# Token-number scatters moved into the loop over further blocks, and the last norm ahead of that loop, in a decoder layer with a mixture of experts

## The chip, the cores and the metric

The kernel runs on one core of a Trainium2 chip. The metric is device microseconds of one execution; the time of a kernel is the median of its runs. The engines are named as in the profile: PE (TensorE, matrix products), PEld (its weight loads), DVE (VectorE), ACT (ScalarE), POOL (GpSimd) and SP (SyncE, which issues most DMAs). L268 is the line of a recording helper through which most instructions go, so instructions are told apart by the names of their tiles.

## The reference

One layer of a decoder over 1024 tokens of width 1024 (and 16 learned ones ahead of them): a normalisation, four token mixers, an output projection, a normalisation, a mixture of experts, and a last normalisation. The change lies in the mixture of experts and behind it:

```
def _hier_moe(x, w_grp, b_grp, w_rt, b_rt, w_gate, w_up, w_down):
    ...
    g_sel = jnp.argmax(g_logit, -1)
    ...
    top_val, top_idx = lax.top_k(e_logit, TOP_K_INNER)
    w = jax.nn.softmax(top_val, -1) * p_grp
    e_idx = g_sel[:, None] * EXPERTS_PER_GROUP + top_idx
    ...
    for e in range(N_EXPERTS):
        hid = jax.nn.silu(xf @ w_gate[e]) * (xf @ w_up[e])
        y = y + gate[:, e:e + 1] * (hid @ w_down[e])
...
    h = _layer_norm(DN_ALPHA * h + moe_out, ln2_g[l], ln2_b[l])
return h[:, N_META:]
```

Each token takes two of 16 experts. All tensors are float32; the last normalisation scales by `ln2_g` and adds `ln2_b`.

## The kernel before

**The experts.** After the routing each expert has a first block of up to 192 tokens (`CAP`). `Experts` goes through the 16 experts one after the other. POOL gathers the expert's token rows from DRAM (`xg<-h1d,ix`, two gathers of 96 rows by an indirect DMA, four buffers). PE transposes them (`py<-ident,xg`), ACT and DVE split them into a high and a low part (`xT`), PE multiplies by the gate and up weights (`pg`), ACT and DVE form the hidden layer (`sg`, `th`, `su`) and split it into `hdh` (ACT) and `hdl` (DVE), and PE multiplies by the down weights (`py`). ACT copies the product to `ey`, and SP stores it in the result table `ys` in DRAM (`ys<-ey`, one store for each expert, two for the last two). The weights come in pieces of 512 KB (`raw`), issued by SP as buffers come free; ACT rounds each piece to its high part (`s4h`, `mT0h` and so on), and DVE or POOL subtracts for the low part (`s4l`, `mT0l`).

**Further blocks.** Where an expert has more than 192 tokens, the rest is done by `expert` in a device loop behind the 16 experts (L3016), once for each further block. The number of blocks, `nov`, is worked out on the device. With the inputs of this case it is 0, and no pass of the loop appears in the trace. A pass reads token numbers from the table `ids` in DRAM. `Routing.rest` fills that table with 16 indirect scatters on POOL (`ids<-tki,si`, 128 numbers each); each of them waits until the one before has landed, since all write one table. Behind them it writes a row of 16 numbers by an IOTA on POOL (`oj`), and DVE works out from it which blocks follow (`sl<-inc,oj` and eleven small instructions to `nov`).

**The end.** `ahead` gathers, for five of the eight groups of 128 tokens, the result of each token's first expert (`y<-ys,slot`, all from experts 0 to 14, so that it can run while expert 15 is computed) and adds it to the residual, times its weight. After the loop `finish` gathers the eight second results (`z`) and the three first ones that are left (`x`). DVE adds (L2880, with the sums of the rows; L2849 for the three), ACT squares with sums, takes the root and normalises, POOL multiplies by `ln2_g`, DVE adds `ln2_b`, SP stores. The eighth group is done in two halves.

**What sets the order.** The recording layer `Order` fixes the order of instructions on PE, DVE, ACT and POOL from the order in which generators yield; each engine runs its row in order, so what waits holds up all that stands behind it. `rest` runs beside the experts from the third on, `ahead` when 15 experts are stored. `finish` has an order of its own behind the loop. A program orders SP. The loop is a point at which all engines meet.

## Time and profile before

| | us |
|---|---|
| runs (three) | 1714.13, 1709.41, 1715.12 |
| median | 1714.13 |
| profiled execution | 1709.09 |
| its span | 1707.4 |
| PE busy | 1558.3 (91%) |
| PEld busy | 1320.4 (77%) |
| DVE busy | 1130.8 (66%) |
| ACT busy | 753.0 (44%) |
| POOL busy | 463.0 (27%) |

The span runs from the first to the last instruction; the profiled execution took 1.7 us more than its span. The experts fill about 1365 to 1640 us of it, `ahead`, the loop's empty start and `finish` the rest. Busy shares are means over the whole program, so the stretch in question has to be read by itself.

### The profile page before, as it was taken

What the parts mean: (1) busy time and instruction counts of PE and PEld (TensorE: products, weight loads), DVE (VectorE), ACT (ScalarE), POOL (GpSimd) and SP (SyncE); (2) the same over time, 40 slices, a digit from 0 to 9 for tenths busy, and PEclk for the clock granted to TensorE, in tenths of its full rate; (3) what the DMA queues carried; (4) which work ended last, traced back from release to release, by engine and by line L of the source; (5) the groups of instructions that cost most, each with busy time, mean ns of one, the idle gap of its engine ahead of it and who ended that gap; (6) DMA issues with size and microseconds to landing.
All of it is one profiled execution on the core that took longest, in us unless ns stands there. A gap on an engine that the chain in (4) does not pass through costs nothing. (4 is left out here: it accounts for less than half of the span.)

```text
span 1707.4 us, 27539 instructions
## 1 busy us (share of the span) xinstructions
PE 1558.3 (91%) x9899; PEld 1320.4 (77%) x9899; DVE 1130.8 (66%) x2545; ACT 753.0 (44%) x1519; POOL 463.0 (27%) x578
## 2 busy tenths in 40 slices
PE   4999998999999999999999999988999899699950
PEld 3999898888887777778787777766888778689840
DVE  8345765744589888865565588477576586477558
ACT  4344444445544454425444334331211367467634
POOL 5222227821111111232221221157200223301026
PEclk9999999999999999999999999999999899899985
DMA  7875444342322233262210541377223688699764
GB/s 242 250 215 153 144 141 115 98 121 72 102 69 75 68 96 102 90 191 75 59 35 17 142 120 49 105 242 244 71 87 112 185 237 269 174 283 291 222 195 179
DMA packets 224555, 244.84 MB, mean 143 GB/s; under 512 B 39531, under 2 KB 172557, under 8 KB 224417
## 3 DMA queue, kind: packets, MB, share of 16 engines
q1 hardware_dynamic: 218016, 222.08, 42.9%
q0 software_dynamic: 6400, 20.98, 4.4%
q8 instruction: 79, 1.29, 0.3%
q14 instruction: 60, 0.48, 0.1%
HBM read 168.98 MB, written 74.03 MB: 142 GB/s over the span
## 5 line engine op out<-in xcount | busy, mean ns | idle before, releaser
L268 PE MATMUL pj<-hTl,wh 128*128 128x512 f32 (+3 forms) x1184 | 432.6, 365 | 1.0 <-DVE hTl L268 1.0
L268 PE MATMUL pj<-hTh,wh 128*128 128x512 f32 (+3 forms) x1184 | 432.2, 365 | 0.0
L268 PE MATMUL pj<-hTh,wl 128*128 128x512 f32 (+3 forms) x1184 | 428.5, 362 | 0.0
L268 POOL TENSOR_TENSOR wl<-wr,wh 128x256 fp32r<-128x256 f32 (+1 forms) x177 | 138.0, 796 | 420.3 <-ACT wh L268 415.6
L268 PEld LDWEIGHTS pj<-hTh,wh 128*128 128x128 f32 (+1 forms) x1184 | 223.7, 189 | 26.4 <-issue 2.0
L268 PEld LDWEIGHTS pj<-hTl,wh 128*128 128x128 f32 (+1 forms) x1184 | 223.6, 189 | 26.4 <-issue 1.6
L268 PEld LDWEIGHTS pj<-hTh,wl 128*128 128x128 f32 (+1 forms) x1184 | 223.9, 189 | 23.5 <-issue 1.4
L268 ACT COPY pe<-pj 128x384 f32<-128x384 f32 (+3 forms) x84 | 37.3, 444 | 119.6 <-PE pj L268 81.5
L268 DVE SCALAR_TENSOR_TENSOR sc<-rl,wi,sc 128x512 f32<-128x512 f32 (+3 forms) x77 | 59.8, 776 | 39.8 <-ACT rl L268 36.4
L268 ACT CAST wh<-wr 128x256 fp32r<-128x256 f32 (+1 forms) x240 | 85.1, 402 | 0.1
L268 ACT ACTIVATE pe<-pj 128x512 f32<-128x512 f32 x64 | 38.1, 595 | 100.7 <-PE pj L268 75.0
L268 POOL TENSOR_TENSOR h<-h,g 128x512 f32<-128x512 f32 x46 | 63.7, 1399 | 51.6 <-issue 32.2
L268 PE MATMUL pg<-xT,mT0h 128*128 128x384 f32 x208 | 64.0, 369 | 0.0
L268 POOL DMA_INDIRECT xg<-h1d,ix x32 | 34.3, 1071 | 109.0 <-PE py L268 100.8
L268 ACT ACT_TABLE_LOAD x46 | 59.0, 1283 | 5.8 <-DVE qk L268 2.6
L268 POOL TENSOR_TENSOR sc<-sc,band 128x256 f32<-128x256 f32 (+1 forms) x32 | 24.4, 764 | 121.2 <-DVE sc L268 82.8
L268 PE MATMUL pg<-xT,mT0l 128*128 128x192 f32 x208 | 54.5, 262 | 0.0
L268 DVE TENSOR_TENSOR mT0l<-raw,mT0h 128x1024 fp32r<-128x1024 f32 x36 | 43.4, 1222 | 15.6 <-ACT mT0h L268 15.5
L268 ACT COPY PT<-xb 128x512 f32<-128x512 f32 (+3 forms) x56 | 27.4, 489 | 55.0 <-PE xb L268 52.8
L268 DVE TENSOR_TENSOR xT<-py,xT 128x384 fp32r<-128x384 f32 x64 | 35.2, 553 | 23.3 <-ACT xT L268 23.2
L268 PEld LDWEIGHTS po<-v,PT 128*128 128x128 f32 x352 | 45.8, 191 | 5.7 <-ACT PT L268 2.5
L268 PE MATMUL po<-v,PT 128*128 128x64 f32 x352 | 47.2, 271 | 0.7 <-ACT PT L268 0.7
(638 smaller groups left out, 3779.8 us busy)
## 6 DMA issues: line engine op xcount, KB each, us to landing
wr<-in_w_in_dram SPq DMA_DIRECT2D x59, 512.0 KB
raw<-in_moe_w_gate_dram SPq DMA_DIRECT2D x32, 512.0 KB
raw<-in_moe_w_up_dram SPq DMA_DIRECT2D x32, 512.0 KB
raw<-in_moe_w_down_dram SPq DMA_DIRECT2D x32, 512.0 KB
gtd<-pe SPq DMA_DIRECT2D x52, 256.0 KB
g<-gtd SPq DMA_DIRECT2D x52, 256.0 KB
ys<-ey SPq DMA_DIRECT2D x14, 768.0 KB
ys<-zero SPq DMA_DIRECT2D x8, 960.0 KB
```

What stands on the lines that cost most here:

```text
L268: r = f(*args, **kw)
```

## The change

The scatters go from `Routing.rest` to the body of the loop, and with that are issued only if a pass runs; their numbers (`si`, `tki`) are kept in a pool that lives to the end. The IOTA stays in `rest`. The results of first blocks are now taken for all tokens without regard to the loop: a slot of a further block is replaced by slot 0 with weight 0 (`slot`, `wt`), and a second pair (`slox`, `wx`) holds it for the loop. `ahead` gathers and adds all eight groups of first results, in six buffers, into the residual's own tiles. `finish` runs ahead of the loop: the eight second gathers, adds, norms and stores. In it DVE does both the multiplication and the addition, ACT takes the mean, and POOL only gathers. A pass of the loop ends with `again`, which adds what the further block gave, norms and stores once more.

```diff
-AHEAD = 5
-LAG = 2
+AHEAD = 6
+FAR = 16384
...
+        a, b, so, fs = t("oa"), t("ob8"), t("so", 2), t("fs", 2)
+        nc.vector.tensor_scalar(fs, sf, float(NE * CAP), -float(FAR), op0=OP.is_ge, op1=OP.mult)
+        nc.vector.tensor_add(sf, sf, fs)
+        yield
...
+        nc.vector.tensor_copy(self.slot, fs)
+        nc.vector.tensor_scalar(fs, so, float(FAR), float(NSLOT - 1), op0=OP.add, op1=OP.min)
+        nc.vector.tensor_copy(self.slox, fs)
+        nc.vector.tensor_scalar(fs, so, 0.0, None, op0=OP.is_ge)
...
-        for j in range(8):
-            for i in range(2):
-                nc.gpsimd.indirect_dma_start(out=self.ids, out_offset=bass.IndirectOffsetOnAxis(ap=si[:, j, i:i + 1], axis=0),
-                                             in_=tk[:, j:j + 1], in_offset=None)
-                yield nc.t["tensor"] + 4
...
 def ahead(k, ys, r):
...
+    for j in range(8):
+        if j >= AHEAD:
+            yield from add()
+        y = k.Y.tile([128, D], F32, name="y", bufs=AHEAD)
+        gather(k, ys[0:(NE - 1) * CAP], r.slot[:, j, 0:1], y)
+        pend.append((j, y, nc.end))
         yield 0.0
...
 def finish(k, ys, r, out, W):
...
-    def norm(j):
-        nc.scalar.activation(x[j], x[j], AF.Identity, bias=m[j], scale=v[j])
-        nc.gpsimd.tensor_mul(x[j], x[j], k.gb2[:, 0])
...
+    for j in range(8):
         nc.vector.scalar_tensor_tensor(x[j], y[j], r.wt[:, j, 1:2], x[j], op0=OP.mult, op1=OP.add, accum_out=s[j])
...
+        if j:
+            nc.scalar.activation(y[j - 1], x[j - 1], AF.Identity, bias=b[j - 1], scale=v[j - 1])
+        nc.scalar.activation(m[j], s[j], AF.Copy, scale=-1.0 / D)
         nc.scalar.activation(y[j], x[j], AF.Square, bias=m[j], accum_out=v[j])
         nc.scalar.activation(v[j], v[j], AF.Sqrt, bias=k.eps, scale=1.0 / D)
...
+        if j:
+            nc.vector.tensor_mul(y[j - 1], y[j - 1], k.gb2[:, 0])
+            nc.vector.tensor_add(y[j - 1], y[j - 1], k.gb2[:, 1])
+            nc.sync.dma_start(out[0, (j - 1) * 128:j * 128], y[j - 1])
         nc.vector.reciprocal(v[j], v[j])
...
-        k.nc = nc
-        r = parts[3]
+            k.nc = nc
+            r = parts[3]
+            finish(k, ys, r, out, ctx.enter_context(tc.tile_pool(name="fin1", bufs=1, side="right")))
...
+                for j in range(8):
+                    for p in range(2):
+                        nc.gpsimd.indirect_dma_start(out=ids, out_offset=bass.IndirectOffsetOnAxis(ap=r.si[:, j, p:p + 1], axis=0),
+                                                     in_=r.tki[:, j:j + 1], in_offset=None)
...
-                for j, y in enumerate(k.y):
-                    gather(k, ys, r.slot[:, j, 0:1], y)
-                    first(k, r, j, y)
-        with tc.manual_schedule(engines={E.PE, E.DVE, E.Activation, E.Pool}), tc.tile_pool(name="fin1", bufs=1) as W:
-            finish(k, ys, r, out, W)
+                again(k, ys, r, out, W)
```

How this moves instructions shows on two engines. First POOL, from the last subtraction before the scatters to the IOTA, in the kernel before (`xg<-h1d,ix` gathers token rows, `ids<-tki,si` scatters token numbers):

```order
L268 TENSOR_TENSOR s7l<-raw,s7h 128x1024
L268 DMA xg<-h1d,ix 96x1024 x2
L268 DMA ids<-tki,si 18432x1 x3
L268 DMA xg<-h1d,ix 96x1024 x2
L268 DMA ids<-tki,si 18432x1 x4
L268 DMA xg<-h1d,ix 96x1024 x2
L268 DMA ids<-tki,si 18432x1 x4
L268 DMA xg<-h1d,ix 96x1024 x2
L268 DMA ids<-tki,si 18432x1 x4
L268 DMA xg<-h1d,ix 96x1024 x2
L268 DMA ids<-tki,si 18432x1
L268 IOTA oj 1x16
```

The same place on POOL after the change, and on to the loop (`y` and `z` are the gathers of first and second results):

```order
L268 TENSOR_TENSOR s7l<-raw,s7h 128x1024
L268 DMA xg<-h1d,ix 96x1024 x2
L268 IOTA oj 1x16
L268 TENSOR_TENSOR mT0l_12417<-raw,mT0h_12413 128x1024
L268 DMA xg<-h1d,ix 96x1024 x20
L268 DMA y<-ys,slot 128x1024 x8
L2849 DMA z_16529<-ys,slot 128x1024
L2849 DMA z_16530<-ys,slot 128x1024
L2849 DMA y<-ys,slot 128x1024 x6
```

The sixteen scatters are gone from between the gathers, the IOTA stands behind the first pair of gathers, one subtraction for a weight piece (`mT0l`) has come to POOL, and all 16 gathers of results stand ahead of the loop (L3021, L3022).

Second DVE, in the middle of `finish`, before (`y` and `x` are the sums, `z` the gathered results, `gb` the gain and bias of the last norm):

```order
L2896 TENSOR_TENSOR y_16432<-y_16432,gb_16243 128x1024
L2880 SCALAR_TENSOR_TENSOR x_16813,s_16845<-z_16821,wt,x_16813 128x1024
L2888 RECIPROCAL v_16836<-v_16836 128x1
L2889 TENSOR_TENSOR m_16828<-m_16828,v_16836 128x1
L2883 TENSOR_SCALAR m_16829<-s_16845 128x1
L2896 TENSOR_TENSOR y_16433<-y_16433,gb_16243 128x1024
L2880 SCALAR_TENSOR_TENSOR x_16814,s_16846<-z_16822,wt,x_16814 128x1024
L2888 RECIPROCAL v_16837<-v_16837 128x1
L2889 TENSOR_TENSOR m_16829<-m_16829,v_16837 128x1
L2883 TENSOR_SCALAR m_16830<-s_16846 128x1
L2896 TENSOR_TENSOR y_16434<-y_16434,gb_16243 128x1024
```

And after (`h` is the residual's tile, `y` and `z` the gathered results, reused for the norm):

```order
L2894 SCALAR_TENSOR_TENSOR h_9910,s_16555<-y,wt,h_9910 128x1024
L2901 TENSOR_TENSOR z_16530<-z_16530,gb_16235 128x1024
L2902 TENSOR_TENSOR z_16530<-z_16530,gb_16235 128x1024
L2904 RECIPROCAL v_16547<-v_16547 128x1
L2905 TENSOR_TENSOR b_16563<-m_16539,v_16547 128x1
L2894 SCALAR_TENSOR_TENSOR h_9910,s_16556<-y,wt,h_9910 128x1024
L2901 TENSOR_TENSOR y<-y,gb_16235 128x1024
L2902 TENSOR_TENSOR y<-y,gb_16235 128x1024
L2904 RECIPROCAL v_16548<-v_16548 128x1
L2905 TENSOR_TENSOR b_16564<-m_16540,v_16548 128x1
```

Before, DVE had one instruction with `gb` for each group (L2896), some groups behind the add (L2880); now it has two (L2901, L2902), each group's right behind the next group's add (L2894), and no adds of first results (L2849).

## Rows read from the trace of the kernel before

**Rows 1.** Windows: PE, PEld, DVE, ACT, POOL busy (instructions); PE clock, DMA share, GB/s.

```profile
1386.00:1402.00 16.00, 14.81 (x92) 12.82 (x92) 14.55 (x42) 11.37 (x21) 4.77 (x5) 1.00 0.83 213
...
1470.40:1507.00 36.60, 19.89 (x91) 16.44 (x90) 14.87 (x30) 11.41 (x21) 8.88 (x10) 0.72 0.64 184
...
1523.50:1540.00 16.50, 16.50 (x106) 14.86 (x105) 11.55 (x18) 11.82 (x21) 1.99 (x2) 1.00 0.97 301
```

**Rows 2.** Waits, 1465 to 1505: total us, times, longest.

```profile
PE py L268 <- ACT hdh L268: 11.5, 1, 11.5
...
PE py L268 <- DMA xg<-h1d,ix: 4.9, 1, 4.9
```

**Rows 3.** Timeline of POOL: start, length, instruction, idle before it and releaser.

```profile
1390.84 1.05 POOL L268 DMA_INDIRECT xg<-h1d,ix  x1 [1.29 <-PE py L268]
1398.68 1.08 POOL L268 DMA_INDIRECT ids<-tki,si  x1 [6.78 <-DVE si L268]
...
1486.17 1.00 POOL L268 DMA_INDIRECT ids<-tki,si  x1 [0.30 <-issue]
1487.18 0.14 POOL L268 IOTA oj<- 1x16 f32 x1
```

**Rows 4.** Tile view of tki: its instructions (ns), and what POOL waited for.

```profile
L268 POOL DMA_INDIRECT ids<-tki,si x16: 952/984/1852, 1398.7 to 1486.2; - x16
L268 DVE CAST tki<-tk x1: 167/167/167, 1396.5 to 1396.5; 128x8 int32<-128x8 f32 x1
...
  DMA ids<-tki,si: 57.5, 13
```

**Rows 5.** Timeline of DVE at the long window's end.

```profile
1487.36 0.41 DVE L268 TENSOR_TENSOR sl<-inc,oj 1x256 bf16<-1x256 f32 x1 [19.11 <-POOL oj L268]
```

**Rows 6.** Timeline of SP: four of the stores of results.

```profile
1416.59 0.55 SPq L268 DMA_DIRECT2D ys<-ey  x1
...
1468.66 0.42 SPq L268 DMA_DIRECT2D ys<-ey  x1
...
1505.07 0.62 SPq L268 DMA_DIRECT2D ys<-ey  x1
...
1604.40 0.35 SPq L268 DMA_DIRECT2D ys<-ey  x1
```

**Rows 7.** Timeline of DVE in the last norm.

```profile
1659.80 1.28 DVE L2880 SCALAR_TENSOR_TENSOR y<-z,wt,y 128x1024 f32<-128x1024 f32 x1 [7.60 <-DMA z<-ys,slot]
...
1669.57 8.62 DVE L2880 SCALAR_TENSOR_TENSOR y<-z,wt,y 128x1024 f32<-128x1024 f32 x1
...
1682.31 1.21 DVE L2896 TENSOR_TENSOR y<-y,gb 128x1024 f32<-128x1024 f32 x1
...
1702.26 1.28 DVE L2921 TENSOR_TENSOR x<-x,gb 128x512 f32<-128x512 f32 x2
```

**Rows 8.** Timeline of POOL in the last norm.

```profile
1655.44 0.94 POOL L2844 DMA_INDIRECT z<-ys,slot  x1 [9.68 <-issue]
...
1660.41 1.49 POOL L2844 DMA_INDIRECT z<-ys,slot  x1 [0.30 <-issue]
...
1670.15 6.95 POOL L2893 TENSOR_TENSOR y<-y,gb 128x1024 f32<-128x1024 f32 x3
```

**Rows 9.** Timeline of ACT in the last norm.

```profile
1682.43 1.15 ACT L2884 ACTIVATE z<-x,m 128x1024 f32<-128x1024 f32 x1
...
1683.70 0.30 ACT L2885 ACTIVATE v<-v,eps 128x1 f32<-128x1 f32 x1
...
1695.15 1.52 ACT L2914 ACTIVATE x<-x,m,v 128x512 f32<-128x512 f32 x2 [0.65 <-DVE m L2889]
```

**Rows 10.** DMA, 1645.5 to 1649: queue, packets, MB, share of 16 engines.

```profile
q0 software_dynamic: 295, 1.05, 90.6%
```

**Rows 11.** Timeline of SP: the last two stores of results.

```profile
1646.68 3.10 SPq L268 DMA_DIRECT2D ys<-ey  x2
```

**Rows 12.** Instructions of SP at the loop's line: ns min/median/max, first and last start.

```profile
L3016 SPq EVENT_SEMAPHORE  x21: 17/28/28, 1650.0 to 1655.2; - x21
```

More of the change, by code (lines that the diff above doesn't have):

```diff
@@ L2844, in gather, with add @@
     k.nc.gpsimd.indirect_dma_start(out=y, out_offset=None, in_=ys, in_offset=bass.IndirectOffsetOnAxis(ap=ix, axis=0))
-def first(k, r, j, y):
-    k.nc.vector.scalar_tensor_tensor(y, y, r.wt[:, j, 0:1], k.h1[j // 4][:, j % 4], op0=OP.mult, op1=OP.add)
 def ahead(k, ys, r):
-    k.y = [k.Y.tile([128, D], F32, name=f"y{j}") for j in range(AHEAD)]
-    for j, y in enumerate(k.y):
-        gather(k, ys[0:(NE - 1) * CAP], r.slot0[:, j], y)
+    nc, pend = k.nc, []
+    def add():
+        j, y, t = pend.pop(0)
+        h = k.h1[j // 4][:, j % 4]
+        yield t
+        nc.vector.scalar_tensor_tensor(h, y, r.wt[:, j, 0:1], h, op0=OP.mult, op1=OP.add)
@@ L2858, in ahead @@
+    for j in range(8):
[4 more added lines that the diff above has]
+        pend.append((j, y, nc.end))
         yield 0.0
-    for j, y in enumerate(k.y):
-        yield k.nc.ready[y.tensor.name]
-        first(k, r, j, y)
+    t = k.Y.tile([128, 1], F32, name="t")
+    nc.scalar.activation(t, k.eps, AF.Sqrt)
+    while pend:
+        yield from add()
 def finish(k, ys, r, out, W):
@@ L2879, in add, with rest @@
-    def add(j):
+    x = [k.h1[j // 4][:, j % 4] for j in range(8)]
+    k.y = y = [W.tile([128, D], F32, name=f"z{j}") for j in range(8 - AHEAD)] + [k.Y.tile([128, D], F32, name="y", bufs=AHEAD) for j in range(AHEAD)]
+    m, v, s, b = ([W.tile([128, 1], F32, name=f"{n}{j}") for j in range(8)] for n in "mvsb")
+    for j in range(8):
+        gather(k, ys[0:NE * CAP], r.slot[:, j, 1:2], y[j])
+    def rest(j, cs):
+        for c in cs:
+            nc.scalar.activation(y[j][:, c], x[j][:, c], AF.Identity, bias=b[j], scale=v[j])
+        for c in cs:
+            nc.vector.tensor_mul(y[j][:, c], y[j][:, c], k.gb2[:, 0, c])
+            nc.vector.tensor_add(y[j][:, c], y[j][:, c], k.gb2[:, 1, c])
+            nc.sync.dma_start(out[0, j * 128:j * 128 + 128, c], y[j][:, c])
@@ L2888, in scale @@
         nc.vector.reciprocal(v[j], v[j])
-        nc.vector.tensor_mul(m[j], m[j], v[j])
-    def norm(j):
-        nc.scalar.activation(x[j], x[j], AF.Identity, bias=m[j], scale=v[j])
-        nc.gpsimd.tensor_mul(x[j], x[j], k.gb2[:, 0])
-    def last(j):
-        nc.vector.tensor_add(x[j], x[j], k.gb2[:, 1])
-        nc.sync.dma_start(out[0, j * 128:j * 128 + 128], x[j])
-    for j in range(8):
-        add(j)
-        i = j + AHEAD - LAG
-        if AHEAD <= i < 8:
-            first(k, r, i, x[i])
-        if j:
-            scale(j - 1)
-        stats(j)
-        if j:
-            norm(j - 1)
-        if j > 3:
-            last(j - 4)
@@ new lines, in finish, with again @@
+    rest(7, [slice(0, 512), slice(512, D)])
+def again(k, ys, r, out, W):
+    nc = k.nc
+    m, v, s, b = (W.tile([128, 1], F32, name=n) for n in "mvsb")
+    for j in range(8):
+        h, x, y = W.tile([128, D], F32, name="xo"), W.tile([128, D], F32, name="yo"), k.y[j]
+        gather(k, ys, r.slox[:, j, 0:1], x)
+        nc.vector.scalar_tensor_tensor(h, x, r.wx[:, j, 0:1], k.h1[j // 4][:, j % 4], op0=OP.mult, op1=OP.add)
+        gather(k, ys, r.slox[:, j, 1:2], x)
+        nc.vector.scalar_tensor_tensor(h, x, r.wx[:, j, 1:2], h, op0=OP.mult, op1=OP.add, accum_out=s)
+        nc.vector.tensor_scalar(m, s, -1.0 / D, None, op0=OP.mult)
+        nc.scalar.activation(y, h, AF.Square, bias=m, accum_out=v)
+        nc.scalar.activation(v, v, AF.Sqrt, bias=k.eps, scale=1.0 / D)
+        nc.vector.reciprocal(v, v)
+        nc.vector.tensor_mul(b, m, v)
+        nc.scalar.activation(y, h, AF.Identity, bias=b, scale=v)
+        nc.vector.tensor_mul(y, y, k.gb2[:, 0])
+        nc.vector.tensor_add(y, y, k.gb2[:, 1])
+        nc.sync.dma_start(out[0, j * 128:j * 128 + 128], y)
```

49 lines of the change are left out of this document (11 added, 38 removed).

## The prediction

> **What bounds the kernel now.** I read four views in this order: busy times by stretch, waits of the stretch that stands out, the lists of instructions of the engines named there, and last the end of the program.
>
> The windows cut the loop over the sixteen experts at its stores of results. In most of it TensorE is the bound: 16.50 us busy of 16.50 at clock 1.00, with VectorE at 11.55. One window is different: in 1470.40 to 1507.00 TensorE is busy for 19.89 of 36.60 us, at a mean clock of 0.72 [rows 1]. Its waits there are 11.5 us for hdh, the rounded hidden layer that ScalarE makes, and 4.9 us for a gather of token rows [rows 2]. Both lead to GpSimd. VectorE, which makes hdh's input, stood for 19.11 us at the first line that reads oj, a row of sixteen numbers [rows 5]. The IOTA that writes oj takes 0.14 us and stood on GpSimd behind sixteen scatters of token numbers, the first issued at 1398.68 and the last at 1486.17, just ahead of the IOTA [rows 3]. GpSimd waited 57.5 us, 13 times, for one scatter to land before it issued the next [rows 4]. The scatters are needed only by a pass over a further block, and no pass runs.
>
> What the stall costs: after it, stores of results come every (1604.40 - 1505.07)/6 = 16.555 us. The ten intervals from 1416.59 to 1604.40 took 187.81 us, where ten at that pace are 165.55: 22.3 us too many [rows 6]. A second count gives the same: TensorE does 106 matmul records in 16.50 us at full clock, so the 91 of the long window are 14.2 us of work, and 36.60 - 14.2 = 22.4 [rows 1]. The waits alone are 16.4 [rows 2]; the rest went at the lower clock.
>
> After the experts comes the last norm. Its first VectorE instruction starts at 1659.80, the last starts its two halves at 1702.26 and ends at 1703.54: 43.74 us [rows 7]. VectorE hardly stands idle there, but some of its instructions are stretched: one of 1.28 us took 8.62 while GpSimd ran three multiplications in 6.95, so the two ran one after the other and not side by side [rows 7, 8].
>
> **The change part by part.** (1) *Scatters into the loop body.* No pass runs, so sixteen issues and their waits go, and the IOTA stands right behind a pair of gathers that was issued by 1391.89, a good 5 us before VectorE can ask for oj (the scatters' own numbers were ready only at 1398.68) [rows 3]. The wait of 19.11 us goes whole, and the gathers, no more between scatters, are issued as soon as buffers come free, so the 4.9 go too. What is late next? After the stall TensorE never waited at 16.50 us an expert, with DMA at 0.97 of its time [rows 1]; nothing shows slack in DMA, but nothing waits for it. **-22.3**; at the least the 16.4 of pure waiting.
>
> (2) *More small work in the routing.* Some ten VectorE instructions of 0.17 (a cast of the same shape) [rows 4], and a subtraction of 128x1024 passed from VectorE to GpSimd, where one takes 6.95/3 = 2.3 [rows 8]. They fall about 1386 to 1402, where VectorE is busy for 14.55 of 16.00 and TensorE, at 14.81, already gives way a little [rows 1]. 1.7 us added, 1.2 taken off: **+0.5**, between 0 (cover by TensorE's work) and 2.5 (GpSimd's subtraction late for a matmul).
>
> (3) *The last norm.* GpSimd multiplies no more; VectorE takes those eight multiplications but runs every instruction at its own length. Per block, an add with sums (1.28), a multiplication and an addition (1.21 each) and two small ones (0.17) [rows 4, 7]: 4.04, and as starts overlap the end before by some 0.07, I take 3.9. The first block is a chain: add 1.28, ScalarE's mean about 0.2 (estimated from the square root's 0.30), square to root 1682.43 to 1684.00 = 1.57 [rows 9], two small ones 0.3: 3.4. Inside each block ScalarE's squares and norms (about 3.4) lie under VectorE's 3.9. The last block ends in halves: 0.8 (two in 1.52) [rows 9], then four halves of 0.64 (two in 1.28) [rows 7]: 3.4. Sum 3.4 + 7 x 3.9 + 3.4 = 34.1 against 43.74: -9.6; I allow 0.1 a block for handing over between engines: **-8.9**, between -6 (0.5 us a block) and -9.6. The first adds (three more) stand ahead in the wait for the last results.
>
> (4) *When the last norm starts.* Its first add came 1659.80 - 1655.44 = 4.36 after the issue of its gather [rows 7, 8]. That gather needs the last store of results. Before, the stores issued in the row of 1646.68 [rows 11] moved next to nothing while first gathers were served: 295 packets, 1.05 MB in 3.5 us, nine tenths of DMA's time [rows 10], so 1.75 us for a gather of 0.52 MB. The change puts eight first gathers there instead of five: three more, up to 5.2 us. They no longer end in the loop's handshake, in which GpSimd waited for SP, whose steps end at 1655.2 [rows 12]: about 1.9 us between the landing and 1655.44. I take two thirds of the 5.2, less the 1.9, and some of the issues overlap: **+2.4**, between -1.9 (no store delayed) and +3.3.
>
> (5) *The empty loop behind everything.* SP first waits until all outputs have landed, then the engines step semaphores for some 1.8 us before the closing steps that both kernels have; SP's 21 of them stretch to 1655.2 [rows 12]. Before, this lay in the middle, where (4) has booked it. **+2.1**, 1.5 to 3.5.
>
> (6) *SP.* It reads the number of passes some experts earlier, between two weight loads; VectorE's value is there long before, and the loads behind it run ahead of TensorE. Nothing.
>
> Sum: 1709.09 - 22.3 + 0.5 - 8.9 + 2.4 + 2.1 = **1682.9** for the profiled execution, whose span is 1707.4. The three runs lie 0.3, 5.0 and 6.0 above it; I add some 2: **1685**. Bounds together: best 1709.09 - 22.4 + 0 - 9.6 - 1.9 + 1.5 = 1676.7, worst 1709.09 - 16.4 + 2.5 - 6 + 3.3 + 3.5 = 1696.
>
> **A rule weighed.** A gather issued while VectorE ran an add of two inputs took 1.49 us, where one beside no such work took 0.94 [rows 8]. Half a microsecond for each of eight gathers lies under VectorE's 3.9 a block, so the sum takes nothing for it. The Trainium skill speaks against the change here: GPSIMD Engine Reference, section Key points, has GpSimd contend with VectorE instructions that have two SBUF inputs, and SBUF — State Buffer, section Who interferes with whom, has whoever issues second block fully. By that rule, taken so far that no gather starts under such an instruction, the sum would be that of rival (d), 1727. The trace shows the contention, but 0.55 us of it at a gather, not a lockout.
>
> **The rivals.** *(a) The stall is only partly won.* The experts' pace becomes DMA's: DMA moved 301 GB/s at 0.97 of its time [rows 1], helped by what had piled up in the stall, and without it each expert might wait 0.5 to 0.8 us for weights over ten experts: +5 to +8, **1692**. For it: hardly any DMA time is free. Against: 16.50 busy of 16.50.
>
> *(b) The last norm gives little.* First gathers and stores interfere, ScalarE's chain, not VectorE, sets the block: -3 in place of -8.9 and +3.3 in place of 2.4: **1692**.
>
> *(c) Another instruction takes over the wait for oj*, such as the gathers ahead of the IOTA, which wait for buffers that TensorE frees. If VectorE still loses 15 of its 19.11 us: **1701**. Against: those gathers were issued at 1390.84 [rows 3].
>
> *(d) Slower: VectorE starves GpSimd's gathers.* In the new last norm VectorE runs two-input instructions back to back, and a gather then gets through only in a pause. Under such instructions an issue took 1.49 [rows 8] against 0.94 undisturbed. If it were shut out wholly, each gather would be issued only when VectorE has run dry, and a block would cost its 3.9 plus issue and landing, 0.94 + 4.36 = 5.3. It is slower than before once the gain of 29 us is used up: 29/5.3, so from six blocks starved; eight cost 42: **1727**. Against: the 1.49, a delay of half an instruction, and three or four gathers go out before the first add, 4.36 us after the first of them.
>
> *(e) Better:* DMA freed of scatters and of the stall speeds early experts too: **1676**.
>
> **How the numbers follow.** Forecast 0.66 (1677 to 1691 by itself, 1685); (a) 0.11; (b) 0.09; (c) 0.04; (d) 0.03; (e) 0.07. The range is to hold 8 in 10: **1675 to 1696**, which leaves out (c), (d) and the ends of the others. About 0.3%, 5 us here, is what a measurement of this kernel can tell from no change. All cases but (d) are faster by more than that, save a remainder: faster 0.95, same 0.02, slower 0.03.
>
> **What would show it.** In the profile after: no VectorE wait for oj over 1 us; stores of results every 16.6 to 17.4 us throughout and clock 1.00 up to the last expert; the first add of the last norm about 22.3 - 2.4 earlier, near 1640; no VectorE instruction there over 2 us, and about 35 us from the first to the last; some 2 us of semaphore steps behind the landing of the last output. I am wrong in (1) if TensorE's waits for weights or gathers fill the place of the stall, and in (3) and (4) if the gathers' issues stretch beyond 2 us or the last norm starts over 5 us after its results are stored.

## The result and the profile after

The changed kernel takes 1686.70 us (median of four runs, 1685.27 to 1692.52), the one before 1714.62 (four runs). The ratio is 0.9854, with a 95% interval of 0.9825 to 0.9883. The forecast was 1685, the range 1675 to 1696. The profiled execution took 1685.27, its span is 1683.5 against 1707.4: 23.9 us less. Six later runs of the changed kernel had a median of 1691.33 beside 1710.4 of the kernel before on the same chip, a ratio of 0.9873 (0.985 to 0.9896). So the medians differ by 27.9 us the first time and by 19.1 the second, the two profiled executions by 23.8; the table below shows where that spread comes from.

The page of the changed kernel, its span and its busy times by engine:

```profile
span 1683.5 us, 27555 instructions
...
PE 1550.8 (92%) x9899; PEld 1315.7 (78%) x9899; DVE 1127.1 (67%) x2550; ACT 756.6 (45%) x1527; POOL 428.5 (25%) x555
```

VectorE's busy time hardly moved although it took over eight multiplications; GpSimd's fell from 463.0 to 428.5.

The stores of results on SP (start, length), the first three and the fourteenth, answer to [rows 6]:

```profile
1383.00 0.36 SPq L268 DMA_DIRECT2D ys<-ey  x1
...
1400.78 0.35 SPq L268 DMA_DIRECT2D ys<-ey  x1
...
1418.68 0.34 SPq L268 DMA_DIRECT2D ys<-ey  x1
...
1600.86 0.34 SPq L268 DMA_DIRECT2D ys<-ey  x1
```

From the third to the fourteenth they come every (1600.86 - 1418.68)/11 = 16.56 us, with no gap. The windows of the changed kernel, with the columns of [rows 1], show the same:

```profile
1400.78:1418.68 17.90, 16.81 (x106) 14.84 (x105) 15.69 (x31) 12.69 (x22) 7.23 (x3) 1.00 0.83 267
1468.35:1484.91 16.56, 16.56 (x106) 14.92 (x105) 11.64 (x17) 11.72 (x21) 1.83 (x2) 1.00 0.97 285
```

Where the long window had TensorE busy for 19.89 of 36.60 us at clock 0.72, it is now busy throughout at 1.00. Only the first of these windows has a rest: 1.09 us.

The timeline of GpSimd where the scatters stood, against [rows 3] (start, length, instruction, idle before and what ended it):

```profile
1392.38 1.51 POOL L268 DMA_INDIRECT xg<-h1d,ix  x1 [1.71 <-PE py L268]
1393.91 0.14 POOL L268 IOTA oj<- 1x16 f32 x1
1402.73 5.10 POOL L268 TENSOR_TENSOR mT0l<-raw,mT0h 128x1024 fp32r<-128x1024 f32 x1 [8.68 <-ACT mT0h L268]
```

VectorE's timeline at the place of [rows 5]:

```profile
1402.23 0.41 DVE L268 TENSOR_TENSOR sl<-inc,oj 1x256 bf16<-1x256 f32 x1
...
1405.84 2.02 DVE L268 TENSOR_SCALAR ob<-ob 1x16 f32<-1x16 f32 x1
```

The IOTA is done at 1394.05, VectorE asks for oj at 1402.23 and waits for nothing. Two lengths are new: 5.10 us for a subtraction on GpSimd and 2.02 for an operation on 16 numbers on VectorE.

The last norm on VectorE, its first add, its longest wait after that, the last group's add and the last half, against [rows 7]:

```profile
1640.26 1.28 DVE L2894 SCALAR_TENSOR_TENSOR h<-z,wt,h 128x1024 f32<-128x1024 f32 x1 [1.65 <-DMA z<-ys,slot]
...
1643.42 0.16 DVE L2904 RECIPROCAL v<-v 128x1 f32<-128x1 f32 x1 [1.87 <-ACT v L2899]
...
1668.06 1.28 DVE L2894 SCALAR_TENSOR_TENSOR h<-y,wt,h 128x1024 f32<-128x1024 f32 x1
...
1675.14 0.69 DVE L2890 TENSOR_TENSOR y<-y,gb 128x512 f32<-128x512 f32 x1
```

No instruction is over 1.3 us. From 1640.26 to 1675.83 it is 35.57 us, against 43.74. The wait of 1.87 is the first group's chain through ScalarE.

I cut each profiled execution at five points that can be read on its timelines: the first and the fourteenth store of results on SP, the start of the last hdl on VectorE (expert 15's hidden part), the first add of the last norm, and the end of VectorE's last instruction. In us; the time from the fourteenth store to hdl was 20.47 to 20.49 in all and is left out:

| kernel | first store at | first to 14th store | hdl to last norm | last norm | end | span |
|---|---|---|---|---|---|---|
| before | 1382.05 | 238.89 | 18.38 | 43.74 | 3.86 | 1707.4 |
| changed | 1383.00 | 217.86 | 18.92 | 35.57 | 7.67 | 1683.5 |
| e1, IOTA first | 1381.38 | 234.95 | 18.56 | 44.72 | 3.81 | 1703.9 |
| e2, scatters moved only | 1385.40 | 216.79 | 18.59 | 43.86 | 3.87 | 1689.0 |
| e3, scatters back | 1379.74 | 241.37 | 20.70 | 35.58 | 9.03 | 1706.9 |
| e4, GpSimd multiplies | 1382.12 | 217.71 | 22.00 | 40.42 | 7.68 | 1690.4 |
| e5, loop first | 1387.36 | 217.71 | 25.98 | 36.86 | 3.11 | 1691.5 |
| e6, no loop | 1380.92 | 217.69 | 19.90 | 35.58 | 3.24 | 1677.8 |
| e7, subtraction on VectorE | 1385.57 | 221.74 | 20.20 | 35.62 | 7.70 | 1691.3 |
| e8, seven ahead | 1385.47 | 217.69 | 20.24 | 35.74 | 7.68 | 1687.3 |
| e9, norm in two instructions | 1386.51 | 217.65 | 20.21 | 32.03 | 7.82 | 1684.7 |
| e10, the same, loop first | 1386.98 | 217.67 | 23.39 | 34.85 | 3.54 | 1686.9 |
| e11, changed again | 1387.70 | 217.67 | 20.81 | 35.57 | 7.67 | 1689.9 |
| e12, scatters apart | 1389.02 | 222.23 | 19.63 | 43.65 | 3.88 | 1698.9 |

The change is 217.86 - 238.89 = -21.03 in the experts, +0.54 to the last norm, -8.17 in it, +3.81 behind it, and +0.95 ahead of the first store. That last one is not the change's: the first store comes anywhere from 1379.74 to 1389.02 in kernels that are practically alike up to there, and in the changed kernel itself at 1383.00 and at 1387.70. This column spreads the median times by several us, so the experiments are read by the others. How far those can be trusted shows where kernels have the same code: 217.65 to 217.86 in the experts, 35.57 to 35.62 in the last norm, 7.67 to 7.70 behind it, but 18.92 to 22.00 from hdl to the last norm.

### The profile page after: what moved, and what is told of

It reads as the page before. It is cut to its first block, busy times and chain, and to the rows that moved or that the text cites. A ratio compares the mean times of both kernels' runs of the same rounds, so it can differ in the third digit from the quotient of the medians.

```text
span 1683.5 us, 27555 instructions
## 1 busy us (share of the span) xinstructions
PE 1550.8 (92%) x9899; PEld 1315.7 (78%) x9899; DVE 1127.1 (67%) x2550; ACT 756.6 (45%) x1527; POOL 428.5 (25%) x555
## 5 line engine op out<-in xcount | busy, mean ns | idle before, releaser
L268 DVE TENSOR_TENSOR wl<-wr,wh 128x256 fp32r<-128x256 f32 x63 | 39.1, 640 | 12.6 <-ACT wh L268 12.6
```

Source lines behind the costliest of these rows:

```text
L268: r = f(*args, **kw)
```

## The experiments

**Does the wait for oj make the stall?** One instruction moves:

```diff
+        nc.gpsimd.iota(oj, [[1, 16]], base=0, channel_multiplier=0, allow_small_or_imprecise_dtypes=True)
         for j in range(8):
             for i in range(2):
                 nc.gpsimd.indirect_dma_start(out=self.ids, out_offset=bass.IndirectOffsetOnAxis(ap=si[:, j, i:i + 1], axis=0),
...
-        nc.gpsimd.iota(oj, [[1, 16]], base=0, channel_multiplier=0, allow_small_or_imprecise_dtypes=True)
```

> The kernel before with one instruction moved: the IOTA that writes oj stands ahead of the sixteen scatters on GpSimd; the scatters stay. My theory, that VectorE's wait for oj made most of the stall: that wait (19.11 us) goes, the gathers of token rows that stand between scatters stay late and keep a wait of 5 to 7 us on TensorE, so the kernel gains 15 to 18 us: 1697 to 1700. Rival, that the scatters themselves (their DMA, or the gathers they delay) made the stall: gain of 5 at the most, 1709 or more, with TensorE's wait now put down to a gather. Rival, that the experts' pace becomes DMA's once the stall is gone: TensorE waits for weight pieces, 1702 to 1707.

Measured: 1705.64 us (ratio 0.9944, 0.9919 to 0.9968), and in the experts 234.95 us, only 3.9 less than before. The stores of results on SP, the two with the gap between them (start, length):

```profile
1488.29 0.42 SPq L268 DMA_DIRECT2D ys<-ey  x1
...
1517.00 0.34 SPq L268 DMA_DIRECT2D ys<-ey  x1
```

TensorE's wait for gathers (total us, times, longest):

```profile
PE py L268 <- DMA xg<-h1d,ix: 12.7, 2, 11.9
```

What GpSimd waited for at the scatters (total us, times):

```profile
  DMA ids<-tki,si: 68.5, 15
```

The wait for oj is gone, and a gap of 28.71 us between two stores is there all the same: TensorE now waits 12.7 us for gathers of token rows (11.9 of it at once) that stand on GpSimd behind scatters, and at that the scatters' chain takes longer than before, with its last scatter issued at 1498.2 instead of 1486.17. My 15 to 18 us were wrong. I read it so that the two waits lay over one another: while VectorE was held, the experts stood, and most of the lateness of the gathers (4.9 us of waiting before, 12.7 now) was not yet missed.

**Are the scatters the whole of it?**

```diff
-        for j in range(8):
-            for i in range(2):
-                nc.gpsimd.indirect_dma_start(out=self.ids, out_offset=bass.IndirectOffsetOnAxis(ap=si[:, j, i:i + 1], axis=0),
...
         with tc.For_i(0, nv, 1) as i:
+                for j in range(8):
+                    for p in range(2):
+                        nc.gpsimd.indirect_dma_start(out=ids, out_offset=bass.IndirectOffsetOnAxis(ap=r.si[:, j, p:p + 1], axis=0),
```

> The kernel before with the scatters alone moved into the loop's body (their numbers kept in a tile that lives to the end); first adds, last norm and loop as before. My theory: step (1) alone is worth 22, no added small work (the added 2.1 us of the change belong to the new instructions of the routing and to a subtraction on GpSimd, which this kernel may get too): 1691 to 1694. Rival, that a good part of the gain came from the rest of the change: 1698 or more.

Measured: 1691.88 us (ratio 0.9858, 0.9815 to 0.9901). First and fourteenth store on SP:

```profile
1385.40 0.36 SPq L268 DMA_DIRECT2D ys<-ey  x1
...
1602.19 0.34 SPq L268 DMA_DIRECT2D ys<-ey  x1
```

216.79 us, 22.10 less than before, while last norm and end are as before. This is step (1) alone. By the times it is also nearly all of the change: this ratio, 0.9858, lies beside the 0.9854 and 0.9873 of the whole change. What the rest wins and loses is told apart only in the columns of the table.

**And back.** The changed kernel with the scatters in the routing again:

```diff
+        for j in range(8):
+            for i in range(2):
+                nc.gpsimd.indirect_dma_start(out=self.ids, out_offset=bass.IndirectOffsetOnAxis(ap=self.si[:, j, i:i + 1], axis=0),
...
         nc.gpsimd.iota(oj, [[1, 16]], base=0, channel_multiplier=0, allow_small_or_imprecise_dtypes=True)
```

> The changed kernel with the scatters put back ahead of the IOTA in the routing, and out of the loop's body; last norm and loop as changed. My theory: the stall is back whole, VectorE waits 17 to 20 us for oj, +20 to +23: 1706 to 1710. Rival, that the last norm and the order at the end carry the gain: 1695 or less.

Measured: 1714.73 us, a ratio of 1.0006 (0.9979 to 1.0032); more than I gave it. In the experts it is 241.37, 23.5 more than the changed kernel. VectorE's wait for oj and TensorE's for hdh are there as in [rows 2, 5] (total us, times, longest):

```profile
DVE sl L268 <- POOL oj L268: 17.0, 1, 17.0
```

TensorE's:

```profile
PE py L268 <- ACT hdh L268: 17.2, 3, 15.9
```

The last norm is 8.2 us shorter here too, but its gain is used up: against before the experts take 2.5 us more, the last norm starts 2.3 later, and the end is 5.2 longer, 1.4 more than the changed kernel's. Nearly all of that is GpSimd's closing DRAIN (an instruction at the program's end; ns min/median/max, first and last start), which has 3980 ns in the changed kernel:

```profile
L3056 POOLq DRAIN  x3: 46/103/5289, 1700.8 to 1706.6; - x3
```

With the scatters in place the rest of the change is worth nothing.

**What of a scatter holds the others up, its wait or its transfer?** Kernel e1, with each scatter writing a table of its own, so that none has to wait for the one before:

```diff
-                nc.gpsimd.indirect_dma_start(out=self.ids, out_offset=bass.IndirectOffsetOnAxis(ap=si[:, j, i:i + 1], axis=0),
+                nc.gpsimd.indirect_dma_start(out=self.k.apart[2 * j + i], out_offset=bass.IndirectOffsetOnAxis(ap=si[:, j, i:i + 1], axis=0),
```

> The kernel of e1 (IOTA ahead of the sixteen scatters, all else as before), with each scatter writing a table of its own, so that none waits for the one before to land; the table that a pass would read stays unfilled. In e1 TensorE waited 12.7 us for gathers of token rows that stood on GpSimd between scatters, and from the first to the fourteenth store of results it took 234.95 us, against 216.79 with no scatters. My theory, that the serial waits of the scatters hold up GpSimd's row, not their work: 216.5 to 218.5 from first to fourteenth store, no wait for gathers, and 1690 to 1694. Rival, that the scatters' transfers themselves (128 numbers of four bytes each) hold up the gathers or the weights: 225 or more, 1700 or more.

Measured: 1693.92 us (ratio 0.9883, 0.9842 to 0.9925), 222.23 us in the experts: neither figure, but 12.7 of the 18.2 us that e1 has over e2 are gone, and TensorE waits for no gather. That was the chain of waits. The 5.4 that stay go with the DMA engines' time, as far as the windows show. (The time lies within my 1690 to 1694, but the profiled execution, at 1700.58, was the slowest of four.) Windows over two experts from the second store on, in which scatters are issued here; first this kernel's (columns as in [rows 1]):

```profile
1407.38:1445.98 38.60, 36.16 (x220) 31.88 (x219) 23.27 (x34) 24.59 (x43) 15.01 (x14) 0.96 1.02 236
```

The window of e2:

```profile
1404.11:1436.57 32.46, 32.46 (x205) 29.18 (x204) 25.56 (x43) 24.33 (x43) 6.98 (x5) 1.00 0.97 291
```

ScalarE's waits in this kernel's window:

```profile
ACT s6h L268 <- DMA raw<-in_moe_w_up_dram: 3.5, 1, 3.5
...
ACT mT0h L268 <- DMA raw<-in_moe_w_up_dram: 2.8, 1, 2.8
```

The DMA engines are busy all the time in both (1.02, 0.97), but move 236 GB/s with the scatters and 291 without. ScalarE waits for weight pieces, TensorE's clock falls to 0.96 on the way, and 220 matmul records take 38.60 us where 205 take 32.46. GpSimd is busier too, 15.01 us against 6.98, and what that costs was not held apart.

**Do VectorE and GpSimd run one after the other?** The changed kernel, with GpSimd multiplying by the gain in seven of eight groups:

```diff
-            nc.vector.tensor_mul(y[j - 1], y[j - 1], k.gb2[:, 0])
-            nc.vector.tensor_add(y[j - 1], y[j - 1], k.gb2[:, 1])
...
+            nc.gpsimd.tensor_mul(y[j - 1], y[j - 1], k.gb2[:, 0])
+        if j > 1:
+            last(j - 2)
```

> The changed kernel, where in the last norm GpSimd does seven of the eight multiplications by the gain again, with the addition one group later on VectorE. Theory, that two-input instructions of VectorE and GpSimd run one after the other: a group costs VectorE's 2.5 plus GpSimd's 2.3 plus 0.3 of small ones, 5.1 instead of the 4.06 now, so the last norm takes 40 to 43 us instead of 35.6, and the kernel 1691 to 1694; VectorE's instructions there show lengths over 2 us. Rival, that they overlap freely and the 8.62 of the kernel before was an exception: a group costs ScalarE's 3.1, the last norm takes 29 to 31, and the kernel 1680 to 1683.

Measured: 1693.73 us (ratio 0.9865, 0.9837 to 0.9892), the last norm 40.42 us, 4.56 a group where I gave 5.1. The end of one group on VectorE, the addition and the product of two columns (start, length, instruction):

```profile
1652.61 1.21 DVE L2894 TENSOR_TENSOR z<-z,gb 128x1024 f32<-128x1024 f32 x1
...
1654.75 1.28 DVE L2909 TENSOR_TENSOR b<-m,v 128x1 f32<-128x1 f32 x1
```

GpSimd's timeline:

```profile
1652.83 3.19 POOL L2905 TENSOR_TENSOR z<-z,gb 128x1024 f32<-128x1024 f32 x1 [1.38 <-ACT z L2900]
```

The addition ends at 1653.82. The multiplication, which had started at 1652.83, ends 2.20 us later, at 1656.02, which is about its length alone (2.3, [rows 8]). The product of two columns of 128, 0.16 us elsewhere, started at 1654.75 and ends with it, at 1656.03. In these rows a two-input instruction of one engine stands still while one of the other runs. VectorE's reciprocal at 1654.56, with one input, took its usual 0.16 us beside the multiplication. This is what the Trainium skill, SBUF — State Buffer, section Who interferes with whom, says of two-input instructions, and the trace agrees: 3.19 = 0.99 of waiting + 2.20.

**Where do the 3.8 us at the end come from?** The loop between first adds and last norm (its body leaves out the adding up of a pass's results):

```diff
-            finish(k, ys, r, out, ctx.enter_context(tc.tile_pool(name="fin1", bufs=1, side="right")))
...
         with tc.For_i(0, nv, 1) as i:
...
-                again(k, ys, r, out, W)
+        with tc.manual_schedule(engines={E.PE, E.DVE, E.Activation, E.Pool}), tc.tile_pool(name="fin1", bufs=1, side="right") as W:
+            finish(k, ys, r, out, W)
```

> The changed kernel with the loop between the first adds and the last norm, as before; the loop's body leaves out the adding up of what a pass gives. In the changed kernel 7.67 us lie between VectorE's last instruction and the span's end, 3.81 more than before: semaphore steps of the loop until 1679.6, and GpSimd's closing DRAIN of 3.98 that begins only behind them. My theory: both are hidden again, that end falls to 3.9, and the first add of the last norm comes 1 to 2.5 us later after expert 15: 1683.5 to 1686, a net gain of 1 to 3 us against the change. Rival, that the DRAIN costs its 4 us wherever the loop stands: the end stays at 6 us or more, and the kernel 1687 to 1689.

And the kernel without the loop:

```diff
-        nv = nc.values_load(k.nov[0:1, 0:1], min_val=0, max_val=MAXOV)
-        with tc.For_i(0, nv, 1) as i:
...
```

> The changed kernel without the loop: passes over further blocks are left out, and so is the load of their number. My theory: the end after VectorE's last instruction falls from 7.67 to 3.5 to 4, nothing else moves: 1682 to 1684. Rival, that the end is set by the last output's landing alone (2.8 us of store and 1 of closing steps) and the DRAIN is bound to it: 5.5 or more remains, 1685 or more.

Measured: e6 1683.66 us (ratio 0.9842, 0.9799 to 0.9886), its end 3.24 us; e5 1692.03 us (0.9863, 0.9827 to 0.99), its end 3.11. So the loop costs the end 4.4 to 4.6 us, and the DRAIN is not bound to the landing of the last output. But e5 starts its last norm 7.06 us later than the changed kernel's profile, where I had 1 to 2.5. The chain of waits of e5 at that place (start, us, what):

```profile
1630.31 11.93 DMA y<-ys,slot
...
1643.19 3.00 DMA ys<-ey
```

Ahead of its first step the loop waits until all first gathers have landed, and SP issues the second half of expert 15's results only behind the loop's steps, at 1643.19: the order of SP had changed too. The gain at the end is lost ahead.

**The subtraction that passed to GpSimd.** It goes back to VectorE:

```diff
-            (nc.gpsimd if self.aside else nc.sooner(1024) if pool_lo else nc.vector).tensor_sub(lo, raw, hi.bitcast(F32))
+            (nc.gpsimd if self.aside else nc.sooner(1024) if pool_lo and not hasattr(self.k, "aside") else nc.vector).tensor_sub(lo, raw, hi.bitcast(F32))
```

> The changed kernel with one subtraction for a weight piece (mT0l, 128x1024) taken back from GpSimd to VectorE. On GpSimd it took 5.10 us, more than twice an undisturbed one, and TensorE waited 1.09 us for hdl right behind it. My theory: the engines stood in each other's way there; from the first to the fourteenth store of results it is 216.8 us instead of 217.9, and the kernel 1685 to 1686.5. Rival, that VectorE is full there and the subtraction costs it as much: 217.9 or more.

Measured: 1692.12 us (ratio 0.9874, 0.9839 to 0.9909), 221.74 us in the experts: 3.9 worse, not 1 better. VectorE's instruction for which TensorE waits:

```profile
1416.98 0.55 DVE L268 TENSOR_TENSOR hdl<-th,hdh 128x384 fp32r<-128x384 f32 x1
```

TensorE's timeline:

```profile
1414.91 0.47 PE L268 MATMUL py<-s8h,hdh 128*96 128x512 f32 x1 [1.20 <-ACT hdh L268]
...
1417.58 0.47 PE L268 MATMUL py<-s8h,hdl 128*96 128x512 f32 x1 [1.97 <-DVE hdl L268]
```

The window of five us behind it, columns as in [rows 1]:

```profile
1417.00:1422.00 5.00, 4.42 (x13) 3.05 (x14) 1.62 (x5) 1.69 (x3) 0.00 (x0) 0.68 0.89 299
```

With the subtraction in VectorE's row the recorded order puts two more of them (s6l, s7l) ahead of hdl, so hdl comes at 1416.98 and TensorE waits 1.20 and 1.97 us; after that its clock is 0.68. VectorE was full there, and GpSimd's slow 5.10 us were the cheaper way.

**First gathers and the last store.**

```diff
-    for j in range(8):
+    for j in range(7):
...
+        if j == 0:
+            gather(k, ys[0:NE * CAP], r.slot[:, 7, 0:1], f)
```

> The changed kernel with seven first gathers ahead and the eighth behind the first second gather, its add in the gap that VectorE has in the first group of the last norm (1.87 us). In the changed kernel the last store of results lands 7.08 us after its issue, where it took 4.1 with five first gathers. My theory, that each first gather ahead of it costs it 1 to 1.6 us: it lands 1 to 1.6 earlier, the first add of the last norm follows, and the last norm itself takes no longer: 1685 to 1686. Rival, that the landing is not the gathers' doing: no change in the landing, and the eighth gather makes the second one later, 1687 to 1688.

Measured: 1685.8 us (ratio 0.9834, 0.9801 to 0.9868). From hdl to the last norm 20.24 us, within the 18.92 to 22.00 of kernels with eight. The last store landed 6.84 us after ScalarE's last copy, where it took 6.47 to 8.21 in kernels with eight, so the 1 to 1.6 us that I gave one gather are not told apart from their spread; the last norm took 35.74, so the added add fitted the gap.

**A faster last norm.** VectorE does (sum + mean) x gain in one instruction and x 1/root + bias in a second, and ScalarE normalises no more:

```diff
-            nc.scalar.activation(y[j - 1], x[j - 1], AF.Identity, bias=b[j - 1], scale=v[j - 1])
...
-            nc.vector.tensor_mul(y[j - 1], y[j - 1], k.gb2[:, 0])
-            nc.vector.tensor_add(y[j - 1], y[j - 1], k.gb2[:, 1])
+        nc.vector.scalar_tensor_tensor(x[j][:, c], x[j][:, c], m[j], k.gb2[:, 0, c], op0=OP.add, op1=OP.mult)
...
+            nc.vector.reciprocal(b[j - 1], v[j - 1])
...
+        nc.vector.scalar_tensor_tensor(y[j][:, c], x[j][:, c], b[j], k.gb2[:, 1, c], op0=OP.mult, op1=OP.add)
```

> The changed kernel with another last norm: VectorE takes (sum + mean) times gain in one instruction and times the root's inverse plus bias in a second, so ScalarE's normalising and one small product go, and the second group's add no longer waits for the first group's chain. My theory, that VectorE's row sets the last norm: 3.8 us a group and a start of 3.2, so 30.5 to 32 us instead of 35.6, the rest as in the changed kernel: 1681 to 1684. Rival, that the gathers of second results set the pace once VectorE is faster: 34 us or more, 1685 or more.

Measured: 1686.51 us (ratio 0.9859, 0.9837 to 0.9881), beside 1691.33 (0.9873, 0.985 to 0.9896) of the changed kernel on the same chip; the two intervals overlap. The last norm takes 32.03 us, 3.5 less. One group:

```profile
1651.32 1.28 DVE L2893 SCALAR_TENSOR_TENSOR h<-y,wt,h 128x1024 f32<-128x1024 f32 x1
...
1652.52 1.28 DVE L2886 SCALAR_TENSOR_TENSOR h<-h,m,gb 128x1024 f32<-128x1024 f32 x1
...
1653.91 1.28 DVE L2889 SCALAR_TENSOR_TENSOR z<-h,b,gb 128x1024 f32<-128x1024 f32 x1
```

From this add to the next group's, at 1655.11, it is 3.79 us, as expected. The time did not reach the 1681 to 1684 that I gave; the profile's first store came at 1386.51, 3.5 us behind the changed kernel's.

The same with the loop ahead, a pass adding its results to the residual, and the last store issued by ScalarE:

```diff
-                again(k, ys, r, out, W)
+                more(k, ys, r, i, W)
+        with tc.manual_schedule(engines={E.PE, E.DVE, E.Activation, E.Pool}), tc.tile_pool(name="fin1", bufs=1, side="right") as W:
+            finish(k, ys, r, out, W)
...
-                                nc.sync.dma_start(self.ys[e * CAP + b * HB:e * CAP + (b + 1) * HB], y[:, b])
+                                (nc.scalar if b and e == NE - 1 else nc.sync).dma_start(self.ys[e * CAP + b * HB:e * CAP + (b + 1) * HB], y[:, b])
```

> The kernel of the run before with the loop ahead of the last norm: a pass adds its results to the residual itself, and the last store of results is issued by ScalarE, since SP held it behind the loop where the loop stood first. My theory: the end after VectorE's last instruction falls from 7.7 to 3.1 to 3.9, and the loop's steps cost 1.9 to 2.5 ahead of the second gathers: 1678 to 1681. Rival, that the loop ahead costs 5 or more, as it did with the store behind it: 1683 or more.

Measured: 1688.22 us (ratio 0.9861, 0.9841 to 0.9882). The end is 3.54, but the start came at 23.39 and the last norm took 34.85. GpSimd's first two gathers of second results:

```profile
1641.11 1.54 POOL L2849 DMA_INDIRECT z<-ys,slot  x1 [7.75 <-SPq L3012]
1649.58 1.03 POOL L2849 DMA_INDIRECT z<-ys,slot  x1 [6.93 <-issue]
```

The first went out ahead of the loop's steps, the second 8.47 us later, behind them: the loop waited for that gather to land, at 1647.07 by the chain of waits, before its steps went on. Against the run before, the last norm starts 3.18 us later and takes 2.82 more, 6.0 together, while the end is 4.28 shorter: the rival of 5 us or more holds. Of all these kernels with the loop, e9 has the shortest last norm, but no run shows it faster than the changed kernel beyond the spread of runs.

**The changed kernel again.**

> The changed kernel once more, beside the two others. From expert 15's last hidden part (hdl) to the first add of the last norm it took 18.92 us in its profile and 19.9 to 22.0 in four kernels with the same code there; in most of those TensorE's clock was lower over the last products (a mean of 0.76 where the changed kernel's profile has 1.00). My theory: this varies from one execution to the next, and a second profile may show 0.76 and 20 to 21 us. Rival, that it belongs to the code: 18.9 again, clock 1.00. Time 1685 to 1689 either way.

Measured: 1691.33 us. Seven us from the last hdl on, in the first profile of the changed kernel and in this one (columns as in [rows 1], the clock third from the end):

```profile
1621.34:1628.34 7.00, 5.93 (x24) 3.72 (x24) 4.18 (x4) 3.71 (x6) 5.37 (x6) 1.00 0.85 291
```

In its second profile:

```profile
1625.85:1632.85 7.00, 6.98 (x24) 4.68 (x24) 4.16 (x4) 2.92 (x5) 5.26 (x6) 0.76 0.96 302
```

The clock is 1.00 in the one and a mean of 0.76 in the other, with the same code: it varies by execution, as I expected. The start of the last norm hangs on it only in part. It came after 18.92 and 20.81 us in these two: ScalarE's last copy ended 6.56 and 7.99 us after hdl, which is 1.43 of the 1.89 between them. But in e7, whose clock was 1.00 as well, it came after 20.20, since the last store took 8.21 us to land there instead of 7.08.

## Why the prediction was right, step by step

**(1) Scatters, -22.3: right in size, too simple in cause.** e2 measures -22.10. The text put most of it down to VectorE's wait for oj, and counted the 4.9 us of late gathers beside it. e1 shows that the wait for oj by itself is worth 3.9: with it gone 18 of the 22 us stay, 12.7 of them waits for gathers behind the chain of scatters (e12 takes these away) and 5.4 with the scatters themselves. So the two waits were two covers over one delay: sixteen scatters in a chain, 57.5 us of waiting on an engine whose row holds what two others need. The count over ten intervals gave the right total since the change takes the scatters away whole.

**(2) Small work, +0.5: measured +1.1** (217.86 against e2's 216.79), within its bounds. It is one wait of TensorE, which e2 does not have and e11 has again (1.08):

```profile
1412.71 0.47 PE L268 MATMUL py<-s8h,hdl 128*96 128x512 f32 x1 [1.09 <-DVE hdl L268]
```

The subtraction took 5.10 us on GpSimd instead of 2.3, beside VectorE's row. It ends at 1407.83 and VectorE's stretched operation on 16 numbers at 1407.86, together as in e4; that the two shut each other out here is likely, but was not measured apart. e7 shows that the other choice was worse by 3.9. The first two intervals between stores, 17.78 and 17.90 us, are over the 17.4 that the text named as a sign.

**(3) The last norm, -8.9: measured -8.17.** 4.06 us a group, where the step has 3.9 + 0.1, and the first group's start costs 3.44, to which the text gave 3.4. The last group is longer: 7.77 us from 1668.06 to 1675.83, where the step has 4.0 + 3.4. e4 shows the reason behind the step: GpSimd's multiplications were not help but time taken from VectorE.

**(4) The start of the last norm, +2.4: measured +0.54, and +2.4 against a profile with the same clock.** The step's own terms do not give its figure: two thirds of 5.2, less 1.9, is 1.6. The mechanism is there. In the chain of waits of the changed kernel (start, us, what):

```profile
1627.93 7.08 DMA ys<-ey
...
1635.79 4.29 DMA z<-ys,slot
```

In its second profile, e11:

```profile
1633.87 7.37 DMA ys<-ey
```

The last store takes 7.08 us from ScalarE's last copy to its landing; alone it took 3.00 (e5). Like is compared with like in e11, where the clock over the last products is a mean of 0.76, as in the kernel before: 20.81 - 18.38 = 2.43. There the store lands 7.37 us after the last copy; in the kernel before the copy ended at 1649.44, and GpSimd's last steps of the loop began at 1653.54 with the store landed, so it took 4.1 at the most. Against that 0.8 us instead of 1.9 pass until the next gather. In the first profile the clock of 1.00 brought the last copy 1.43 us forward, and store and gather took 0.46 less; that is why it has only +0.54.

The reading of [rows 10], that a store moves next to nothing beside gathers, holds only for its first few us. From 1630 to 1632 the queue of the stores moved 0.03 MB in the changed kernel, from 1632 to 1634 it moved 0.34 MB beside 0.49 MB of gathers. The 1.28 us in which ScalarE loads its table for the square root, now between its last copies, cost nothing: the last copy starts 5.98 us after hdl with it (changed kernel, e7) and 5.97 without (e12), all three at clock 1.00.

The seven kernels with the changed kernel's code there (changed, e3, e4, e6, e7, e9, e11) have a mean of 20.39 from hdl to the last norm; the four with five first gathers and the loop ahead (before, e1, e2, e12) have 18.79. At the clock of 0.76 it is 20.72 (e3, e4, e6, e9, e11) against 18.51 (before, e1, e2); at 1.00 there are only the changed kernel's 18.92 and e7's 20.20 against e12's 19.63, too few to tell. In the seven the last copy ends 6.56 us after hdl (clock 1.00) or 8.0 to 8.1, the store lands 6.47 to 8.21 us later, and from the gather's issue to the add it is 4.47 to 5.42. What spreads the store and the gather is left open.

**(5) The empty loop, +2.1: measured +3.81, over its upper bound of 3.5.** This is the term that was most mis-sized against its bounds. SP's steps of the loop, GpSimd's closing DRAIN in the changed kernel, and the same in the kernel before (ns min/median/max, first and last start):

```profile
L3022 SPq EVENT_SEMAPHORE  x21: 17/28/28, 1676.4 to 1679.5; - x21
```

GpSimd's DRAIN in the changed kernel:

```profile
L3054 POOLq DRAIN  x3: 46/103/3980, 1678.7 to 1683.3; - x3
```

And in the kernel before:

```profile
L3048 POOLq DRAIN  x3: 46/109/9261, 1696.7 to 1707.1; - x3
```

GpSimd's last multiplication there:

```profile
1698.41 2.24 POOL L2917 TENSOR_TENSOR x<-x,gb 128x512 f32<-128x512 f32 x1
```

The steps take 1679.5 - 1676.4 = 3.1 us, part of which lies over the last output's landing. GpSimd's own steps end at 1678.5, and its DRAIN runs for 3.98 us from 1678.7 on, to within 0.8 us of the span's end. In the kernel before it started at 1696.7, under GpSimd's last multiplications, and lasted 9.26 us: it was over at 1706.0, 5.3 us after the last of them ended (1700.65) and 1.4 us ahead of the span's end, and so was hidden. The text counted the steps of the engines and left out what each engine does after them, though the closing instructions of GpSimd are there in the trace of the kernel before, among the rows of L3048. e6 and e5 show the cost: without the loop, or with the loop ahead, the end falls by 4.4 and 4.6 us.

**(6) SP, nothing: right, but not for the reason given.** VectorE's value was not there long before: SP waited 0.9 us for nov and read it at 1409.7, as soon as VectorE had written it. TensorE waited for no weight piece behind it.

**The rivals.** (a) did not come about: in the experts TensorE never waited for weights, though DMA was at 0.95 to 1.01 of its time in nine of the thirteen intervals between stores (0.58 to 0.83 in the first two and the last two). (b): the last norm gave what was expected. (c): VectorE waits for nothing at oj. (d): gathers under VectorE's row in the changed kernel (start, length):

```profile
1640.99 1.37 POOL L2849 DMA_INDIRECT y<-ys,slot  x1 [0.30 <-issue]
...
1643.91 1.88 POOL L2849 DMA_INDIRECT y<-ys,slot  x1 [0.30 <-DVE b L2905]
```

The longest took 1.88 us and no add after the first waited for its gather, so a gather is held up for an instruction and not for a row. The Trainium skill's sentence on contention (GPSIMD Engine Reference, section Key points) is thus borne out, at 0.4 to 0.95 us a gather, without the price of (d).

The 1685 was met at 1686.7, in part by luck. For the profiled execution the sum gave 1682.9, and it took 1685.27. (1) and (2) together brought 0.8 less than forecast, (3) 0.7 less, (5) cost 1.7 more and the way to the first store 0.95 more; (4) cost 1.9 less, of which 1.4 is the clock of that one execution. The 2 us added for the median over the profiled execution were 1.4.

## What to carry to other kernels

A row of indirect DMAs that all write one table is a chain of landings on the engine that issues them, and all that stands behind it in that engine's row is late; look for every reader of that row, since removing the wait that the profile names can leave the next one in its place. Two-input work on VectorE and two-input work on GpSimd took turns here, so sharing out the last norm between them lost 4.9 us (e4). Where VectorE's row is full and another engine waits for something in it, GpSimd's slower instruction can still be the cheaper one (e7). An empty device loop was paid for at both places tried: in the middle by its wait for gathers under way and its steps (e5, e10), at the very end by its steps and by the DRAIN that GpSimd could otherwise have done early.

## What the runs showed of the hardware

- **TensorE's clock after the same wait is not the same in every execution.** The last products of expert 15 start after 1.99 us of waiting in the changed kernel and in its second profile:

```profile
1621.36 0.47 PE L268 MATMUL py<-s4h,hdh 128*96 128x512 f32 x1 [1.99 <-ACT hdh L268]
```

In the second profile:

```profile
1625.87 0.65 PE L268 MATMUL py<-s4h,hdh 128*96 128x512 f32 x1 [1.99 <-ACT hdh L268]
```

Over the next seven us the granted clock is 1.00 in the changed kernel, e7 and e12 and a mean of 0.76, part of it at the lower of the two levels, in the other eleven profiles. ScalarE's last copy then ends 8.0 to 8.1 us after hdl instead of 6.56. No run shows what decides it.

- **GpSimd's closing DRAIN** takes 3.98 us in the six profiles in which it stands behind the loop and no scatter ran, though in the changed kernel GpSimd's last gather was issued 31 us before. In e3, with the sixteen scatters, it takes 5.29. Where it starts early the same two lengths follow GpSimd's last multiplication: 5.3 us in the kernel before, e1 and e12, 4.0 in e2, without scatters. There it is hidden. No run shows what it does in that time.

- **A store waits among gathers.** With first gathers under way, a store of 384 KB took 7.08 us to land in the changed kernel and 6.47 to 8.21 in six others, against 3.00 alone.

- **Scatters of four-byte numbers take DMA time out of proportion to their bytes:** in e12 236 GB/s were moved at a share of 1.02, against 291 at 0.97 in e2 without them.
